# First chunk of six column groups ahead of the rest, a shorter look-ahead, and a row moved out of a load buffer

## The chip, the cores and the metric

The kernel runs on one core of one Trainium2 chip. The metric is the device time of one execution in microseconds (us). A core has five engines with instruction streams of their own that work in program order and wait for each other by semaphores: TensorE (PE in the profile, PEld its weight loads), VectorE (DVE), ScalarE (ACT), GpSimd (POOL) and SyncE (SP), which here issues all transfers.

## The reference, cut to what matters

One decoder layer in float32: a sequence of 256 rows, width 2048. The change lies in the first lines of it: the conditioning vector `c` gives a shift and a scale, the normalised input times the scale plus the shift is `h`, and `h` is multiplied with a wide matrix of which the kernel takes fourteen groups of 512 columns first.

```python
def hybrid_layer(x, c, w_ada, b_ada, norm_pre_w, w_in, ...):
    shift, scale, gate = jnp.split(jax.nn.silu(c) @ w_ada + b_ada, 3, axis=-1)
    h = rms_norm(x, norm_pre_w) * (1.0 + scale[:, None]) + shift[:, None]
    proj = h @ w_in
    (gdn_qkv, gdn_a, gdn_b, gdn_z, ml_qk, ml_v, ml_i, ml_f, ml_o, ml_z, gate_a, gate_b) = jnp.split(
        proj, np.cumsum(IN_SPLITS)[:-1].tolist(), axis=-1)
    ...
    merged = jax.nn.sigmoid(gate_a) * y_a + jax.nn.sigmoid(gate_b) * y_b
    out = merged @ w_out
    return x + gate[:, None] * rms_norm(out, norm_post_w)
```

## The kernel before

**Three products for one.** Each float32 operand is split into a rounded part and a rest (`split`, L167: ACT casts the rounded part, `whi`, L168; DVE or POOL subtracts it from the original to give the rest, `wlo`, L169). `mm3` (L215) then issues three matmuls of 512 columns: `h_hi` with `whi`, `h_hi` with `wlo`, `h_lo` with `whi`. `split_w` (L173) gives four of five subtractions of the start to POOL, the fifth to DVE.

**The stream.** `Stream` (L62) holds units in the order in which they were added. A unit is a load (one or two transfers into one of three buffers `raw` of 128 x 2048 numbers), its pieces of up to 1024 columns to be prepared (`prep_w`, L183), and their use on PE. `run` prepares pieces as long as no more than `ahead` (3) of them are prepared and not yet used, then issues the use of the oldest. As every engine works in program order, this also fixes what stands behind what on ACT, DVE and POOL. A load is issued as soon as the buffer three units before it is done with.

**The start.** The width 2048 is 16 chunks of 128 (index `k`). The row of `c` is loaded into one partition of a buffer of the ring `ar` (`crow`, L263), goes through Silu on ACT, and four PE matmuls spread it over all partitions (`csil`, L272). The input `x` lies in `xs`; its two halves of 128 rows are squared, summed and scaled by the root (`x_scale`, L289, ACT), and each pair of chunks is turned by four PE transposes and copied back by ACT (`x_turn`, L293, tile `xps`). For each chunk two rows blocks of `w_ada` (for the shift and the scale; 32 units of 1 MB, three buffers `ar`) are multiplied with `csil` and summed by DVE (L344). With both sums `h_chunk(k)` (L319) makes `sh`, `s1`, `hf` and `h_hi` on ACT and `h_lo` on POOL.

**The fourteen groups.** Their products with all 16 chunks are made in five blocks of chunks, `BLOCKS = ((0, 2), (2, 2), (4, 4), (8, 4), (12, 4))`, as first chunk and count. Within a block each group in turn gets its matmuls into two of four PSUM banks (`jtile`, L209, tiles `pn`), one for each half of 128 rows. After the first block ACT copies the two banks to `part[g]` (L403), after a later one DVE adds them to it (L405). In a block of two chunks one unit of 1 MB holds two groups. `PACE` says how many `w_ada` units are added before a block's first and last unit. In the stream the first ten chunks of `x` are turned ahead of the first group (`x_chunks(0, 6)` and `x_chunks(6, 10)`), the other six between later units. What comes after the fourteen groups is not touched by the change.

Of the kernel before, what the change touches and what calls it, by code (L numbers as in the profile page):

```python
# [7 lines left out]
F32 = mybir.dt.float32  # L8
F32R = mybir.dt.float32r
AF = mybir.ActivationFunctionType  # L10
ALU = mybir.AluOpType
# [105 lines left out]
def hybrid_layer_kernel(  # L117
# [91 lines left out]
    def jtile(nm):  # L209
        return pj.tile([P, 512], F32, name=nm, tag="pj")  # L210
# [49 lines left out]

    pcs = ExitStack()
    csil = pcs.enter_context(tc.tile_pool(name="pcs", bufs=1, space=PSUM)).tile([P, D], F32, name="csil")
    crow = sp.tile([P, D], F32, name="crow", tag="ar", bufs=ADA_BUFS)[0:1]  # L263
    SP.dma_start(crow, c_row)
    for b in range(2):
        SP.dma_start(xs[:, b], x[b * P:(b + 1) * P])
    SP.dma_start(ident, consts[:, 0:128])
    bat = const("bat", b_ada_t, [P, 32])
    npre = const("npre", npre_t, [P, KC])
    A.activation(crow, crow, AF.Silu)  # L270
    for q in range(4):
        T.matmul(csil[:, q * 512:(q + 1) * 512], one_row, crow[:, q * 512:(q + 1) * 512], start=True, stop=True)  # L272
    late_c = {}

    def late_consts():
# [25 lines left out]
    def x_chunks(k0, k1):  # L301

        x_scale(k0)
        for k in range(k0, k1, 2):
            if k + 2 < k1:
                x_scale(k + 2)
            x_turn(k)
    x_chunks(0, 6)


    bnp = sp.tile([P, KC], F32, name="bnp")
# [7 lines left out]
    def h_chunk(k):  # L319

        A.activation(sh[:, k:k + 1], ad[:, k:k + 1], AF.Identity, bias=bat[:, k:k + 1])
        A.activation(s1[:, k:k + 1], ad[:, KC + k:KC + k + 1], AF.Identity, bias=bnp[:, k:k + 1],
                     scale=npre[:, k:k + 1])
        hf = sp.tile([P, S], F32, name="hf", tag="hf", bufs=2)
        A.activation(hf.rearrange("p (b t) -> p b t", b=2), xs[:, :, k * P:(k + 1) * P], AF.Identity, bias=sh[:, k:k + 1], scale=s1[:, k:k + 1])
        split(hf, h_hi[:, k], h_lo[:, k], G)

    stream = Stream(load_w, side)
    BLOCKS = ((0, 2), (2, 2), (4, 4), (8, 4), (12, 4))
    PACE = (4, 9.5, 16.5, 26, 32, 32)  # L330
    due = []

    def h_chunks(k):

        while due and due[0] <= k:
            h_chunk(due.pop(0))

    def ada_units():

        adders = []  # L340
        for k in range(KC):
            for pt in range(2):
                def prep(h, raw, k=k, pt=pt):
                    V.scalar_tensor_tensor(raw, raw, 1.0, csil, op0=ALU.mult, op1=ALU.mult,  # L344
                                           accum_out=ad[:, pt * KC + k:pt * KC + k + 1])
                    if 4 <= 2 * k + pt < 8:
                        j = 2 * (2 * k + pt)
                        if j > 8:
                            x_turn(j)
                        if j < 14:  # L350
                            x_scale(j + 2)
                    h_chunks(k - 1)
                    if pt == 1:
                        due.append(k)
# [24 lines left out]
        G.memset(y0, 0.0)  # L379

    def add_start_groups(bi):
        k0, nk = BLOCKS[bi]
        lastb = bi == len(BLOCKS) - 1
        adders, parts_ = [], []
        for g in range(len(START)):
            st_ = {}

            def use(h, hi, lo, g=g, st_=st_):
                if h == 0:
                    st_["ps"] = [jtile(f"pn{i}") for i in range(2)]  # L390
                for kc in range(min(2, nk - 2 * h)):
                    kr = h * 2 + kc
                    k = k0 + kr
                    h_chunks(k)
                    o = kc * 512
                    for b in range(2):
                        mm3(st_["ps"][b], h_hi[:, k, b * P:(b + 1) * P], h_lo[:, k, b * P:(b + 1) * P],
                            hi[:, o:o + 512], lo[:, o:o + 512], kr == 0, kr == nk - 1)

            def after(g=g, st_=st_):  # L400
                for b in range(2):
                    if bi == 0:
                        A.copy(part[g][:, b], st_["ps"][b])  # L403
                    else:
                        V.tensor_tensor(part[g][:, b], st_["ps"][b], part[g][:, b], op=ALU.add)  # L405
                if bi == len(BLOCKS) - 2 and g == 3:
                    late_consts()
                if lastb:
                    pt = part[g].rearrange("p b c -> p (b c)")
                    A.activation(pt, pt, AF.Silu if g in (9, 11, 13) else AF.Sigmoid)  # L410
                    if g < 8:
                        SP.dma_start(gate_dr[g], part[g])
                    elif g % 2:
                        V.tensor_tensor(part[g], part[g], part[g - 1], op=ALU.mult)
                        SP.dma_start(gate_dr[8 + (g - 8) // 2], part[g])
                    if g == NG - 1:
                        branches_open()
            parts_.append((w_in[START[g]][:, k0 * 512:(k0 + nk) * 512], use, after))
        if nk == 2:
            for g in range(0, NG, 2):  # L420
                def use2(h, hi, lo, g=g):
                    parts_[g + h][1](0, hi, lo)
                    parts_[g + h][2]()
                adders.append(lambda g=g, use2=use2:
                              stream.add((parts_[g][0], parts_[g + 1][0]), prep_w, use2))
        else:
            for src, use, after in parts_:
                adders.append(lambda src=src, use=use, after=after:
                              stream.add(src, lambda h, raw: prep_w(h, raw, nk * 512), use, (nk + 1) // 2, after))
        return adders  # L430


# [72 lines left out]
        stream.add(w_ab, prep_w, use, after=lambda: side.add(gates(st_["ps"])))  # L505

    ada = ada_units()
    NG = len(START)
    ia = 0
    for bi, (k0, nk) in enumerate(BLOCKS):  # L510
        if bi == len(BLOCKS) - 1:
            add_ab()
        fs = add_start_groups(bi)
        for j, f in enumerate(fs):
            ahead = PACE[bi] + (PACE[bi + 1] - PACE[bi]) * j / len(fs)
            while ia < len(ada) and ia < ahead:
                ada[ia]()
                ia += 1
            f()
# [795 lines left out]
```

## Time and profile before

| what | value |
|---|---|
| time, median of 3 runs | 1634.56 us (1633.07 to 1636.01) |
| the profiled execution, its own time | 1634.3 us |
| its span, first to last instruction | 1632.5 us |
| PE busy | 1595.8 us, 98% of the span |
| ACT, DVE, POOL busy | 57%, 70%, 15% of the span |
| granted TensorE clock, mean | 0.997 |

The span is 1.8 us shorter than the time of the same execution; the rest lies outside the instructions. A busy share is that of an engine over the whole span; idle time of an engine matters only where the chain that ends last runs through it. In the rows further down, a row of the timeline has the start and the duration of an instruction in us, and in brackets how long the engine sat idle before it and who ended that. Matmuls are pipelined: the duration of one is longer than the distance to the next, and it is the distance that counts.

### The profile page before, as it was taken

The page shows a single profiled execution, that of the slowest core. Times are in us where ns is not written, and L with a number is a line of the kernel's source. Part 1 is how long each engine was busy: PE and PEld are TensorE (multiplying, and loading weights), DVE is VectorE, ACT ScalarE, POOL GpSimd, SP SyncE. Part 2 cuts the span into 40 slices and gives each one's busy share as a digit, 9 for nine tenths or more (in the row PEclk, how much of TensorE's full clock was granted, in tenths as well). Part 3 has the DMA queues.
Part 4 walks back from the last instruction along what each step waited for, and adds up shares of the span by engine and source line. Part 5 has one row for each costly group of instructions (what it writes and reads, how often), then busy time and mean ns, then how long its engine had stood idle before and what let it go on. Part 6 is the DMA issues. An engine that isn't in the chain of part 4 may idle for free.

```text
span 1632.5 us, 25436 instructions
## 1 busy us (share of the span) xinstructions
PE 1595.8 (98%) x9844; PEld 1398.7 (86%) x9844; DVE 1137.3 (70%) x1793; ACT 937.5 (57%) x1496; POOL 241.7 (15%) x191
## 2 busy tenths in 40 slices
PE   6999999999999999999999999999999999999997
PEld 4888887799998999999898989889988788888886
DVE  5585556665678787969686969685878556756654
ACT  7744446665655575666666666665565544444443
POOL 3877760000000010000000000000100000100101
PEclk9999999999999999999999999999999999999999
DMA  9998775765454555454546464646888668766572
GB/s 370 387 364 321 280 272 180 259 245 187 166 197 165 183 175 185 165 184 160 185 161 197 162 198 152 193 167 247 299 301 310 236 235 301 275 233 252 194 278 103
DMA packets 96259, 372.37 MB, mean 228 GB/s; under 512 B 26261, under 2 KB 46213, under 8 KB 58249
## 3 DMA queue, kind: packets, MB, share of 16 engines
q1 hardware_dynamic: 96138, 370.75, 63.9%
q8 instruction: 77, 1.26, 0.3%
q14 instruction: 44, 0.36, 0.1%
HBM read 354.40 MB, written 16.31 MB: 227 GB/s over the span
## 4 chain that ended last, share of the span: by engine, by line
PE 78%; issue 13%; DVE 3%; ACT 2%; DMA 2%; POOL 1%; SPq 0%; DVEq 0%; POOLq 0%; ACTq 0%
PE pn L217 34%; PE pt L217 27%; PE py L217 8%; DVE wlo L169 1%; ACT whi L168 1%; POOL mg L1123 1%; PE psa L217 1%; DMA raw<-in_dram 1%; PE mq L766 1%; PE mz L774 1%; PE mp L741 1%; PE pt L848 0%; DMA ar<-in_dram 0%; PE po L811 0%; PE pc L801 0%
## 5 line engine op out<-in xcount | busy, mean ns | idle before, releaser
L169 DVE TENSOR_TENSOR wlo<-raw,whi 128x1024 fp32r<-128x1024 f32 x450 | 552.7, 1237 | 273.3 <-ACT whi L168 272.4
L168 ACT CAST whi<-raw 128x1024 fp32r<-128x1024 f32 x514 | 532.0, 1051 | 313.2 <-PE pn L217 145.7
L217 PE MATMUL pt<-h_hi,whi 128*128 128x256 f32 x1280 | 368.1, 288 | 0.0
L217 PE MATMUL pt<-h_hi,wlo 128*128 128x256 f32 x1280 | 362.6, 283 | 1.9 <-DVE wlo L169 1.9
L217 PE MATMUL pt<-h_lo,whi 128*128 128x256 f32 x1280 | 362.0, 283 | 0.0
L217 PE MATMUL pn<-whi,h_hi 128*128 128x512 f32 x896 | 354.3, 395 | 3.5 <-ACT whi L168 3.4
L217 PE MATMUL pn<-wlo,h_hi 128*128 128x512 f32 x896 | 350.5, 391 | 3.0 <-DVE wlo L169 3.0
L217 PE MATMUL pn<-whi,h_lo 128*128 128x512 f32 x896 | 350.4, 391 | 0.0
L217 PEld LDWEIGHTS pt<-h_hi,wlo 128*128 128x128 f32 x1280 | 245.1, 191 | 2.8 <-DVE wlo L169 2.7
L217 PEld LDWEIGHTS pt<-h_hi,whi 128*128 128x128 f32 x1280 | 245.2, 192 | 1.3
L217 PEld LDWEIGHTS pt<-h_lo,whi 128*128 128x128 f32 x1280 | 245.3, 192 | 0.2
L217 PEld LDWEIGHTS pn<-whi,h_hi 128*128 128x128 f32 x896 | 169.1, 189 | 40.1 <-ACT whi L168 3.8
L217 PEld LDWEIGHTS pn<-wlo,h_hi 128*128 128x128 f32 x896 | 169.2, 189 | 38.4 <-DVE wlo L169 4.3
L217 PEld LDWEIGHTS pn<-whi,h_lo 128*128 128x128 f32 x896 | 169.0, 189 | 35.8 <-POOL h_lo L169 0.3
L169 POOL TENSOR_TENSOR wlo<-raw,whi 128x1024 fp32r<-128x1024 f32 x64 | 153.6, 2408 | 44.2 <-ACT whi L168 44.2
L217 PE MATMUL py<-whi,yhi 128*128 128x512 f32 x384 | 150.6, 392 | 0.3 <-ACT vt L953 0.3
L217 PE MATMUL py<-whi,ylo 128*128 128x512 f32 x384 | 149.5, 389 | 0.0
L217 PE MATMUL py<-wlo,yhi 128*128 128x512 f32 x384 | 149.4, 389 | 0.0
L405 DVE TENSOR_TENSOR part<-pn,part 128x512 f32<-128x512 f32 x112 | 74.0, 687 | 48.0 <-PE pn L217 48.0
L168 ACT CAST yhi<-ya 128x512 fp32r<-128x512 f32 x48 | 29.9, 622 | 124.7 <-PE py L217 122.9
L169 DVE TENSOR_TENSOR ylo<-ya,yhi 128x512 fp32r<-128x512 f32 x48 | 33.2, 692 | 90.4 <-ACT yhi L168 88.4
L567 DVE SCALAR_TENSOR_TENSOR qs<-pt,gcv,qs 128x255 f32<-128x255 f32 (+2 forms) x192 | 92.2, 480 | 4.6
(243 smaller groups left out, 1800.5 us busy)
## 6 DMA issues: line engine op xcount, KB each, us to landing
raw<-in_dram SPq DMA_DIRECT2D x259, 1024.0 KB
ar<-in_dram SPq DMA_DIRECT2D x32, 1024.0 KB
raw<-in_dram SPq DMA_DIRECT2D x28, 512.0 KB
ya<-o_dr SPq DMA_DIRECT2D x32, 256.0 KB
gate_dr<-part SPq DMA_DIRECT2D x11, 512.0 KB
gb<-rows SPq DMA_DIRECT2D x20, 256.0 KB
ug<-ud SPq DMA_DIRECT2D x32, 128.0 KB
o_dr<-oT SPq DMA_DIRECT2D x16, 256.0 KB
```

Source lines behind the costliest of these rows:

```text
L168: A.copy(hi, src)
L169: (eng or V).tensor_tensor(lo, src, hi.bitcast(F32), op=ALU.subtract)
L217: T.matmul(ps, l, r, start=start and i == 0, stop=stop and i == 2, skip_group_check=True)
L405: V.tensor_tensor(part[g][:, b], st_["ps"][b], part[g][:, b], op=ALU.add)
L567: V.scalar_tensor_tensor(dst[:, n, sh:], src[:, 0:S - sh], taps(n, 3 - sh), dst[:, n, sh:], op0=ALU.mult, op1=ALU.add)
L741: T.matmul(pss[t][o:o + 32, m * 32:(m + 1) * 32], um(m)[r:r + 32, o:o + 32], yc[r:r + 32, m], start=True, stop=True)
L766: T.matmul(psp[64:128, m * 64:(m + 1) * 64], um(m)[0:64, 64:128], y0[:, m], start=True, stop=True)
L774: T.matmul(psz[0:64, m * 64:(m + 1) * 64], p2[64:128, m], x0[64:128, m, 64:128], start=True, stop=True)
L1123: G.tensor_tensor(mcols(b, hf, cg), mcols(b, hf, cg), s_, op=ALU.add)
```

## The change

The fourteen groups are cut into six (`EARLY`) and eight (`REST`), and the first two blocks are replaced by four: the six with chunk 0 alone, the eight with chunks 0 and 1, the six with chunks 1 to 3, the eight with chunks 2 and 3. The later three blocks stay. Units with one or two chunks hold two groups (0.5 or 1 MB), the six with three chunks one group (0.75 MB). The last two numbers of a block stand in the place of `PACE`. `Stream` starts with `ahead` 1 and goes to 3 with the first use in the second block. The row of `c` goes to two partial-sum tiles instead of an `ar` buffer, as two transfers and two Silus. Four chunks of `x` are turned ahead of the first group instead of ten, the other twelve between later units. The rest `h_lo` of chunk 0 is made on DVE. In the first use of a group, one of the two PSUM copies goes to DVE for all but the first two groups.

```diff
-    crow = sp.tile([P, D], F32, name="crow", tag="ar", bufs=ADA_BUFS)[0:1]
-    SP.dma_start(crow, c_row)
+    crow = [part[4 + i].rearrange("p b c -> p (b c)")[0:1] for i in range(2)]
+    for i in range(2):
+        SP.dma_start(crow[i], c_row[:, i * 1024:(i + 1) * 1024])
...
-    A.activation(crow, crow, AF.Silu)
+    for i in range(2):
+        A.activation(crow[i], crow[i], AF.Silu)
...
-    x_chunks(0, 6)
+    x_chunks(0, 4)
...
-        split(hf, h_hi[:, k], h_lo[:, k], G)
-
-    stream = Stream(load_w, side)
-    BLOCKS = ((0, 2), (2, 2), (4, 4), (8, 4), (12, 4))
-    PACE = (4, 9.5, 16.5, 26, 32, 32)
+        split(hf, h_hi[:, k], h_lo[:, k], V if k == 0 else G)
+
+    stream = Stream(load_w, side, 1)
+    NG, NE = len(START), 6
+    EARLY, REST, ALL = range(NE), range(NE, NG), range(NG)
+
+    BLOCKS = ((EARLY, 0, 1, 1.1, 3.5), (REST, 0, 2, 4, 8), (EARLY, 1, 3, 8, 12), (REST, 2, 2, 12, 16.5),
+              (ALL, 4, 4, 16.5, 26), (ALL, 8, 4, 26, 32), (ALL, 12, 4, 32, 32))
...
-                    if 4 <= 2 * k + pt < 8:
-                        j = 2 * (2 * k + pt)
-                        if j > 8:
+                    j = 2 * (2 * k + pt) - 4
+                    if 2 <= j < 16:
+                        if j > 2:
                             x_turn(j)
...
                         if k == 0:
                             h_chunks(0)
-                            x_chunks(6, 10)
...
+        def after(g, ps):
+            for b in range(2):
+                if k0:
+                    V.tensor_tensor(part[g][:, b], ps[b], part[g][:, b], op=ALU.add)
+                elif g < 2 or b == 0:
+                    A.copy(part[g][:, b], ps[b])
+                else:
+                    V.tensor_copy(part[g][:, b], ps[b])
...
+        per = 1 if nk > 2 else 2
+        for g in groups[::per]:
...
+            def use_piece(h, hi, lo, g=g, st_=st_):
+                for i in range(min(2, per * nk - 2 * h)):
+                    gg, c = g + (2 * h + i) // nk, (2 * h + i) % nk
+                    if c == 0:
+                        st_["ps"] = [jtile(f"pn{i}") for i in range(2)]
+                    use(gg, st_["ps"], c, hi, lo, i * 512)
+                    if c == nk - 1:
+                        after(gg, st_["ps"])
+                if bi == 1:
+                    stream.ahead = 3
```

How the instructions move is shown at three places. On SP, the first loads before, from the first `ar` on (`ar` is a unit of `w_ada`, `raw` one of the groups' columns):

```order
L316 DMA ar<-in_dram 128x2048
L316 DMA ar<-in_dram 128x2048 [waits DMAHW0_49]
L316 DMA ar<-in_dram 128x2048 [waits DMAHW1_49,PE_49,Activation_49]
L316 DMA ar<-in_dram 128x2048 [waits DMAHW2_49,DVE_49]
L163 DMA raw<-in_dram 128x1024 [waits DMAHW3_49]
L163 DMA raw<-in_dram 128x1024 [waits DMAHW4_49]
```

And the same place now:

```order
L319 DMA ar<-in_dram 128x2048 [waits DMAHW0_49]
L319 DMA ar<-in_dram 128x2048 [waits DMAHW1_49]
L163 DMA raw<-in_dram 128x512 [waits DMAHW2_49]
L163 DMA raw<-in_dram 128x512 [waits DMAHW3_49]
L163 DMA raw<-in_dram 128x512 [waits DMAHW4_49]
L163 DMA raw<-in_dram 128x512 [waits DMAHW5_49]
L319 DMA ar<-in_dram 128x2048 [waits DMAHW6_49]
```

The first columns stand behind two units of `w_ada` instead of four, and the third unit waits no longer for PE. On ACT, before, from the cast of the first columns to the copies of the first group (`pn_253` and `pn_254` are its two banks; between the casts stand the parts of the second chunk of `h`):

```order
L168 CAST whi<-raw 128x1024 [waits DMAHW3_49]
L168 CAST whi<-raw 128x1024 [waits DMAHW4_49]
L291 ACTIVATE xs<-xs,rsx 128x256 x2
L321 ACTIVATE sh<-ad,bat 128x1 [waits DVE_49]
L322 ACTIVATE s_102<-ad,bnp,npre 128x1 [waits DVE_49]
L325 ACTIVATE hf<-xs,sh,s_102 128x256 [waits Activation_49]
L168 CAST h_hi<-hf 128x256 [waits Activation_49]
L168 CAST whi<-raw 128x1024 [waits DMAHW6_49]
L168 CAST whi<-raw 128x1024 [waits DMAHW7_49]
L403 COPY part_104<-pn_253 128x512 [waits PE_49]
L403 COPY part_104<-pn_254 128x512 [waits PE_49]
```

And now, from the third cast of columns on:

```order
L404 COPY part_105<-pn_216 128x512 [waits PE_49]
L168 CAST whi<-raw 128x1024 [waits DMAHW7_49,DMAHW0_49]
L404 COPY part_106<-pn_235 128x512 [waits PE_49]
L404 COPY part_107<-pn_245 128x512 [waits PE_49]
L294 ACTIVATE xs<-xs,rsx 128x256 x2
L168 CAST whi<-raw 128x1024 [waits DMAHW2_49]
L404 COPY part_108<-pn_264 128x512 [waits PE_49]
L404 COPY part_109<-pn_274 128x512 [waits PE_49]
L168 CAST whi<-raw 128x1024 [waits DMAHW3_49,DVE_49]
L324 ACTIVATE sh<-ad,bat 128x1 [waits DVE_49]
L325 ACTIVATE s_102<-ad,bnp,npre 128x1 [waits DVE_49]
```

Four casts stood ahead of the first copy; now two do, and from the third on each cast stands behind copies of matmuls that PE has to finish first. On PE, now, where chunk 1 of `h` is first used (group 7, banks `pn_291` and `pn_292`) and the turns of `x` follow:

```order
L217 MATMUL pn_291<-whi,h_hi 128x512 [waits Activation_49]
L217 MATMUL pn_291<-wlo,h_hi 128x512
L217 MATMUL pn_291<-whi,h_lo 128x512 [waits Pool_49]
L217 MATMUL pn_292<-whi,h_hi 128x512
L217 MATMUL pn_292<-wlo,h_hi 128x512
L217 MATMUL pn_292<-whi,h_lo 128x512
L300 MATMUL xps<-con,xs 128x128 [waits DVE_49]
L300 MATMUL xps<-con,xs 128x128 x3
L300 MATMUL xps<-con,xs 128x128 [waits DVE_49,Activation_49]
```

Before, that place had one turn behind the first group and no second one:

```order
L217 MATMUL pn_254<-whi,h_lo 128x512
L297 MATMUL xps<-con,xs 128x128 [waits PE_49]
L297 MATMUL xps<-con,xs 128x128 x3
L217 MATMUL pn_282<-whi,h_hi 128x512 [waits PE_49]
```

The second turn follows the first at once and waits for an ACT instruction that stands behind the first one's copy.

## Rows read from the trace of the kernel before

**Rows 1.** The page: span, and the busy time of PE.

```profile
span 1632.5 us, 25436 instructions
PE 1595.8 (98%) x9844; PEld 1398.7 (86%) x9844; DVE 1137.3 (70%) x1793; ACT 937.5 (57%) x1496; POOL 241.7 (15%) x191
```

**Rows 2.** The chain of work that ended last, from 0 to 120 us: start, us, what.

```profile
22.14 11.00 DMA raw<-in_dram
...
43.39 76.68 PE pn L217 x337
```

**Rows 3.** Busy time in stretches of 5 us: length, then PE, PEld, DVE, ACT, POOL busy (and instructions), granted clock, DMA share, GB/s.

```profile
20.00:25.00 5.00, 1.64 (x6) 0.73 (x4) 4.77 (x5) 2.86 (x5) 0.00 (x0) 1.00 1.01 422
25.00:30.00 5.00, 4.54 (x12) 3.11 (x12) 2.77 (x3) 4.39 (x9) 3.78 (x3) 1.00 1.02 424
30.00:35.00 5.00, 5.00 (x26) 4.15 (x25) 2.30 (x2) 4.52 (x9) 4.73 (x3) 1.00 1.02 424
```

**Rows 4.** What PE waited for from 20 to 290 us: us in total, times, longest.

```profile
PE pn L217 <- ACT whi L168: 3.4, 1, 3.4
PE pn L217 <- DVE wlo L169: 2.1, 2, 1.7
...
PE pn L217 <- ACT part L403: 0.2, 1, 0.2
```

**Rows 5.** Timeline, the first transfers on SP.

```profile
1.19 0.33 SPq L264 DMA_DIRECT2D crow<-in_dram  x1
1.56 0.82 SPq L266 DMA_DIRECT2D xs<-in_dram  x2
4.08 10.90 SPq L316 DMA_DIRECT2D ar<-in_dram  x4
```

**Rows 6.** Timeline of the engines up to the first matmuls of the groups.

```profile
12.32 2.29 DVE L344 SCALAR_TENSOR_TENSOR ar<-ar,csil 128x2048 f32<-128x2048 f32 x1 [1.46 <-DMA ar<-in_dram]
...
17.02 0.39 ACT L322 ACTIVATE s<-ad,bnp,npre 128x1 f32<-128x1 f32 x1 [0.63 <-DVE ar L344]
...
18.08 0.40 ACT L168 CAST h_hi<-hf 128x256 fp32r<-128x256 f32 x1
18.39 1.70 ACT L291 ACTIVATE xs<-xs,rsx 128x256 f32<-128x256 f32 x4
...
23.18 1.04 ACT L168 CAST whi<-raw 128x1024 fp32r<-128x1024 f32 x1 [1.59 <-DMA raw<-in_dram]
...
24.27 0.80 PE L217 MATMUL pn<-whi,h_hi 128*128 128x512 f32 x1 [3.36 <-ACT whi L168]
...
25.53 0.80 PE L217 MATMUL pn<-wlo,h_hi 128*128 128x512 f32 x1 [0.46 <-DVE wlo L169]
...
28.90 0.63 PE L217 MATMUL pn<-whi,h_lo 128*128 128x512 f32 x1
...
29.33 0.47 PE L217 MATMUL pn<-whi,h_hi 128*128 128x512 f32 x1
```

**Rows 7.** Timeline of PE around one turn of `x`, in the dense part.

```profile
35.78 0.39 PE L217 MATMUL pn<-whi,h_lo 128*128 128x512 f32 x1
...
36.02 0.60 PE L297 MATMUL xps<-con,xs 128*128 128x128 f32 x4
...
36.37 0.48 PE L217 MATMUL pn<-whi,h_hi 128*128 128x512 f32 x1
...
36.68 0.40 PE L217 MATMUL pn<-wlo,h_hi 128*128 128x512 f32 x1
```

**Rows 8.** Timeline of ACT in the dense part: a cast of 1024 columns, two PSUM copies, the copy of a turn, the next scaling.

```profile
35.13 1.06 ACT L168 CAST whi<-raw 128x1024 fp32r<-128x1024 f32 x1
36.08 1.08 ACT L403 COPY part<-pn 128x512 f32<-128x512 f32 x2
37.03 0.62 ACT L299 COPY xs<-xps 128x512 f32<-128x512 f32 x1
37.51 0.94 ACT L291 ACTIVATE xs<-xs,rsx 128x256 f32<-128x256 f32 x2
```

**Rows 9.** Groups of POOL instructions, 25 to 110 us: count, busy us, mean ns, idle before.

```profile
L169 POOL TENSOR_TENSOR wlo<-raw,whi 128x1024 fp32r<-128x1024 f32 x26 | 62.3, 2413 | 18.4 <-ACT whi L168 18.3
L169 POOL TENSOR_TENSOR h_lo<-hf,h_hi 128x256 fp32r<-128x256 f32 x7 | 5.3, 752 | 7.0 <-ACT h_hi L168 7.0
```

**Rows 10.** Timeline of DVE in the second block: four adds, then a unit of `w_ada`.

```profile
79.62 2.48 DVE L405 TENSOR_TENSOR part<-pn,part 128x512 f32<-128x512 f32 x4
82.02 2.28 DVE L344 SCALAR_TENSOR_TENSOR ar<-ar,csil 128x2048 f32<-128x2048 f32 x1
```

**Rows 11.** Timeline of PE around its two longest waits of the start.

```profile
285.61 0.50 PE L217 MATMUL pn<-wlo,h_hi 128*128 128x512 f32 x1 [1.68 <-DVE wlo L169]
...
286.18 0.40 PE L217 MATMUL pn<-whi,h_hi 128*128 128x512 f32 x1
286.41 0.39 PE L217 MATMUL pn<-wlo,h_hi 128*128 128x512 f32 x1
...
294.72 0.30 PE L488 MATMUL tp<-con,work 128*128 128x128 f32 x1 [3.60 <-DVE part L405]
...
296.42 0.63 PE L217 MATMUL pn<-wlo,h_hi 128*128 128x512 f32 x1
296.84 0.63 PE L217 MATMUL pn<-whi,h_lo 128*128 128x512 f32 x1
```

More of the change, by code (lines that the diff above doesn't have):

```diff
@@ L269, in hybrid_layer_kernel @@
     npre = const("npre", npre_t, [P, KC])
-    A.activation(crow, crow, AF.Silu)
+    for i in range(2):
+        A.activation(crow[i], crow[i], AF.Silu)
     for q in range(4):
-        T.matmul(csil[:, q * 512:(q + 1) * 512], one_row, crow[:, q * 512:(q + 1) * 512], start=True, stop=True)
+        T.matmul(csil[:, q * 512:(q + 1) * 512], one_row, crow[q // 2][:, (q % 2) * 512:(q % 2 + 1) * 512],
+                 start=True, stop=True)
     late_c = {}
@@ L381, in add_start_groups @@
     def add_start_groups(bi):
-        k0, nk = BLOCKS[bi]
+        groups, k0, nk = BLOCKS[bi][:3]
         lastb = bi == len(BLOCKS) - 1
-        adders, parts_ = [], []
-        for g in range(len(START)):
-            st_ = {}
[L388 to L429, printed above, removed]
+        def use(g, ps, c, hi, lo, o):
+            k = k0 + c
+            h_chunks(k)
+            for b in range(2):
+                mm3(ps[b], h_hi[:, k, b * P:(b + 1) * P], h_lo[:, k, b * P:(b + 1) * P],
+                    hi[:, o:o + 512], lo[:, o:o + 512], c == 0, c == nk - 1)
@@ new lines, in after @@
+        def after(g, ps):
+            for b in range(2):
+                if k0:
[4 more added lines that the diff above has]
+                    V.tensor_copy(part[g][:, b], ps[b])
+            if bi == len(BLOCKS) - 2 and g == 3:
+                late_consts()
+            if lastb:
+                pt = part[g].rearrange("p b c -> p (b c)")
+                A.activation(pt, pt, AF.Silu if g in (9, 11, 13) else AF.Sigmoid)
+                if g < 8:
+                    SP.dma_start(gate_dr[g], part[g])
+                elif g % 2:
+                    V.tensor_tensor(part[g], part[g], part[g - 1], op=ALU.mult)
+                    SP.dma_start(gate_dr[8 + (g - 8) // 2], part[g])
+                if g == NG - 1:
+                    branches_open()
@@ new lines, in add_start_groups @@
+        adders = []
+        per = 1 if nk > 2 else 2
+        for g in groups[::per]:
+            st_ = {}
+            def use_piece(h, hi, lo, g=g, st_=st_):
[8 more added lines that the diff above has]
+                    stream.ahead = 3
+            src = tuple(w_in[START[g + i]][:, k0 * 512:(k0 + nk) * 512] for i in range(per))
+            adders.append(lambda src=src, use_piece=use_piece:
+                          stream.add(src, lambda h, raw: prep_w(h, raw, per * nk * 512), use_piece,
+                                     (per * nk + 1) // 2))
@@ L507, in hybrid_layer_kernel @@
     ada = ada_units()
-    NG = len(START)
     ia = 0
-    for bi, (k0, nk) in enumerate(BLOCKS):
+    for bi, (groups, k0, nk, first, last) in enumerate(BLOCKS):
         if bi == len(BLOCKS) - 1:
@@ L514, in hybrid_layer_kernel @@
         for j, f in enumerate(fs):
-            ahead = PACE[bi] + (PACE[bi + 1] - PACE[bi]) * j / len(fs)
+            ahead = first + (last - first) * j / len(fs)
             while ia < len(ada) and ia < ahead:
```

## Prediction

> **What bounds the kernel now.** I read the page first: PE is busy for 1595.8 of 1632.5 us [rows 1], so only PE's idle time, some 37 us, and its slow matmuls can be won back. Then the chain of waits: from 43.39 us on it is PE itself, 337 matmuls in 76.68 us or 0.2275 us each; before that it runs through a load of columns from 22.14 us on [rows 2]. The stretches show where the idle time lies: PE is busy for 1.64 of 5 us from 20 to 25 us, for 4.54 in the next, and full from 30 us [rows 3]. The waits say that this is nearly all of the start: after the one wait of 3.4 us for the first cast, PE loses 0.2 us to a copy and 2.1 us to `wlo` up to 290 us [rows 4]. So the change can gain only ahead of some 30 us, and whatever it delays behind that point is lost in full, as PE has no slack there.
>
> One thing more about that place. The first matmul of a group starts at 24.27 us, the second at 25.53 us, and up to 29.33 us they follow each other at 0.43 us (28.90 to 29.33) instead of 0.2275 [rows 6]. That is 512 columns at the lower of TensorE's two levels (1.2 GHz), although the granted clock of the stretch reads 1.00 [rows 3]; PE had been mostly idle before.
>
> **The change part by part.**
>
> *The lead.* What ends last ahead of the first group is now the sum of the second `w_ada` unit, not the load of columns. Before, that sum let `s1` start at 17.02 us [rows 6]. The second transfer for the row of `c` costs SP one more issue, 1.56 - 1.19 = 0.37 us [rows 5], and all that follows, `x` and the two units, comes as much later: `s1` at 17.39. From `s1` to the end of `h_hi` it is 18.48 - 17.02 = 1.46 us, and the next ACT instruction starts 18.39 - 17.02 = 1.37 us after `s1` [rows 6]. That is now the cast of the first columns: 18.76 to 19.80 us. They are there in time: the first unit lands at 12.32, now 12.7; behind it the second (1.05 MB) and the columns (0.52 MB) take 3.8 us at some 410 GB/s, the rate at which the queue ran [rows 3], so they land at about 16.5. PE starts 1.09 us after a cast's start [rows 6], at **19.85**, a lead of 4.42 us on 24.27. The second matmul waits for DVE as before (1.26 us later): 21.11.
>
> *What is given back.* The first unit now holds 12 matmuls for one chunk of two groups, the next two units as many, then come units of 24. With `ahead` 1, only the first two pieces are cast before a copy; from the third on each cast stands behind copies on ACT that wait for PE, and its subtraction, nearly always POOL's (2.41 us [rows 9]), comes after that. I follow the order row by row. A cast moves ACT on by 0.95 us, a copy by 0.48, a turn's copy by 0.48, a scaling by 0.47 [rows 8]; a copy's result is there 0.55 after its start.
> - Batch 1: 11 more matmuls at 0.43 us from 21.11 end at 25.8. Its last copy ends at 26.6. The third cast runs to 27.65, POOL's subtraction from 27.7 to 30.1.
> - Batch 2, prepared long before, takes 12 x 0.2275 = 2.7 us: PE is through at 28.5, does one matmul of batch 3 and stands until 30.15: **1.4 us**. Batch 3 ends at 32.65.
> - Piece 4 is cast after two copies and two scalings, from 29.5, and subtracted from 30.6 to 33.0: **0.2 us**. Piece 5 is cast after two copies of batch 3 (32.7 to 33.7) and subtracted by POOL from 33.75 to 36.15.
> - Chunk 1 of `h` stands on ACT behind that cast: 0.2 us for `sh` and 1.46 for the rest give `h_hi` at 35.3. PE, with the six matmuls of chunk 0 done at 34.2, waits **1.1 us**. `h_lo` stands on POOL behind 36.15 and takes 0.75: 36.9; PE has done two more matmuls at 35.8 and waits **1.1 us** again. The piece ends at 37.85.
> - Two turns follow. The second needs a scaling that stands on ACT behind the copy of the first turn, itself behind a copy of the piece just ended: turn 38.3, copy 38.6 to 39.2, scaling from 39.1, second half of the wait at 39.65. PE stands **1.4 us**; the turns are through at 40.15 and PE starts its 49th matmul of the groups.
>
> From there each piece is cast two batches ahead and nothing waits. Before, 36 matmuls stood ahead of the turn at 36.02; the 37th started at 36.37, the 38th at 36.68 [rows 7], so the 49th at 36.68 + 11 x 0.2275 = 39.18. PE is 0.97 us late instead of 4.4 early.
>
> *The turns.* A turn costs dense PE (36.68 - 35.78) - 2 x 0.2275 = 0.45 us [rows 7]. Before, five lay in idle time and two more had passed at this point; now four have. Three more come later: **1.34 us**.
>
> *DVE in the second block of the eight.* A unit of 24 matmuls takes PE 5.46 us. DVE has four adds (2.40 us [rows 10]), 4.5 units of `w_ada` for four of columns (1.125 x 2.28 = 2.57) and about 0.45 of subtractions: 5.4 us, with no room; before it had one unit of `w_ada` for each. And at the seam two stand in a row ahead of a subtraction. Bounds: nothing, and the 1.68 us that PE once stood for such a subtraction at 285.61 [rows 11]. I take 0.5, nearer to nothing, since DVE enters this block with free time.
>
> *Costed at nothing.* The copies that go from ACT to DVE: DVE is busy for 2.3 of 5 us there [rows 3]; uncovered, 0.6 each. The third `w_ada` unit without its wait for PE: it is needed only for chunk 1, whose wait lies elsewhere. The two shorter Silus: `x` and its sums, not `csil`, end last. `h_lo` of chunk 0 on DVE: in the place of an idle 1.46 us [rows 6]; uncovered 0.4. The number of adds and copies stays.
>
> *Sum.* +0.97 + 1.34 + 0.5, less the 0.2 of [rows 4], is +2.6 us on the profiled execution's 1634.3: **1636.9 us**, against the median of 1634.56 +2.3, or 0.14%. A change under 0.2% (3.3 us) is about what cannot be told from none here.
>
> **The rivals.**
>
> *The clock falls again* (the one that ends slower). Between 28.5 and 40 us PE stands five times. If it went back to the lower level at the second stall, the rest of batch 3 would take 11 x 0.2 = 2.2 us more, which moves the copies, casts and subtractions behind it in full, and the six matmuls of the next piece about 1 us more, half hidden by the wait for chunk 1: +3.0, or **1639.9 us**. It decides with the first matmul after 30.15. For and against stand two waits: after 1.68 us of idle PE went on at 286.41 - 286.18 = 0.23 us a matmul, after 3.60 us it fell to 296.84 - 296.42 = 0.42 [rows 11]. The stalls are of at most 1.4 us, nearer to the first. [...]
>
> *The higher level comes early.* With all of batch 1 at 0.2275, it ends at 23.6, the third cast and all behind it move up by 2.2 us, and the time is **1634.7 us**. Against it: from rest PE took until 29.33 before.
>
> *The lead is kept.* If the stalls were covered, for example because a shorter way of the copies lets ACT cast ahead, what remains is 1634.3 - 4.42 + 1.34 - 0.2 = **1631.0 us**. Against it stands the order: the casts are behind the copies, whatever the durations.
>
> *DVE falls behind*: the upper bound of 1.7 instead of 0.5, **1638.1 us**. For it speaks the load of 5.4 in 5.46 us.
>
> **How the numbers follow.** Forecast 0.58 (alone 1635.0 to 1638.8: the steps of ACT and POOL are worth half a us each way, the point at which the clock rises about 1), the clock falls 0.15, early level 0.12, DVE 0.10, lead kept 0.05. The range leaves out the outer parts of the first and the last: 1632.8 to 1640.4. Slower by over 0.2%, above 1637.8: the clock case 0.14, DVE 0.07, a quarter of the forecast 0.15, together 0.36. Faster by over 0.2%, below 1631.3: 0.05. The same: 0.59.
>
> **What would show it.** The first matmul of a group near 19.9 us; a distance of 0.43 us until about 25 us; PE waiting for POOL's `wlo` near 30 us, for `h_hi` and `h_lo` near 35 and 37, for a scaling of `xs` near 39.5; the 49th matmul near 40; then no wait but one for DVE near 88. It is wrong if PE is dense from 28 us, if the distance goes back to 0.43 after 30 us, or if the load of columns ends the wait at 19.9 after all.

## The result and the profile after

| what | before | after |
|---|---|---|
| time, median of 22 runs each | 1635.71 us (1632.57 to 1642.82) | 1638.8 us (1636.38 to 1646.11) |
| ratio after to before | | 1.0019, 95% interval 1.0011 to 1.0028 |
| span of the profiled execution | 1632.5 us | 1637.1 us |

The changed kernel is 3.1 us slower by the medians, 0.19%. The interval, 0.11 to 0.28% or 1.8 to 4.6 us, leaves out zero: with 22 runs of each, a change under 0.2%, which the prediction took for one that cannot be told from none, can be told. The forecast was 1636.9 us, +2.6 on the profiled execution and +2.3 on the median known then, the range 1632.8 to 1640.4. The two executions that were profiled lie 4.6 us apart, more than the medians; where the other 1.7 us lie is told below.

The page of the changed kernel, span and PE, answers to [rows 1]:

```profile
span 1637.1 us, 25454 instructions
PE 1596.1 (97%) x9844; PEld 1398.8 (85%) x9844; DVE 1149.2 (70%) x1807; ACT 931.8 (57%) x1488; POOL 241.0 (15%) x192
```

PE does the same 9844 instructions in the same busy time (1596.1 against 1595.8 us). So what was lost is idle time of PE. What PE waited for from 20 to 290 us (us in total, times, longest) says where:

```profile
PE pn L217 <- ACT whi L168: 5.6, 1, 5.6
PE pn L217 <- DVE wlo L169: 2.1, 2, 1.7
PE pn L217 <- DVE part L402: 1.3, 1, 1.3
PE pn L217 <- POOL wlo L169: 1.1, 1, 1.1
PE xps L300 <- ACT xs L294: 1.1, 1, 1.1
PE pn L217 <- ACT h_hi L168: 1.0, 1, 1.0
PE pn L217 <- POOL h_lo L169: 0.9, 1, 0.9
```

Against [rows 4] five waits are new: for POOL's `wlo`, `h_hi`, `h_lo` and a scaling of `xs`, and one of 1.3 us for DVE's addition at L402 (L405 before). A last wait, of 0.4 us near 267 us, is left out here; every kernel of this document has it. The first row is the wait for the first cast; it ends 4.3 us earlier than before, which the length of the wait doesn't tell (it counts from the last turn, and fewer turns lie there now). The timeline shows when each ends (start, duration, idle time before and who ended it):

```profile
17.50 0.39 ACT L325 ACTIVATE s<-ad,bnp,npre 128x1 f32<-128x1 f32 x1 [2.14 <-DVE ar L350]
...
18.86 1.99 ACT L168 CAST whi<-raw 128x1024 fp32r<-128x1024 f32 x2
...
19.95 0.79 PE L217 MATMUL pn<-whi,h_hi 128*128 128x512 f32 x1 [5.64 <-ACT whi L168]
...
21.21 0.80 PE L217 MATMUL pn<-wlo,h_hi 128*128 128x512 f32 x1 [0.47 <-DVE wlo L169]
...
23.08 0.63 PE L217 MATMUL pn<-whi,h_lo 128*128 128x512 f32 x1
...
23.51 0.55 PE L217 MATMUL pn<-whi,h_hi 128*128 128x512 f32 x1
...
23.90 0.40 PE L217 MATMUL pn<-wlo,h_hi 128*128 128x512 f32 x1
24.13 0.39 PE L217 MATMUL pn<-whi,h_lo 128*128 128x512 f32 x1
...
25.05 0.40 PE L217 MATMUL pn<-whi,h_hi 128*128 128x512 f32 x1
...
25.73 1.05 ACT L168 CAST whi<-raw 128x1024 fp32r<-128x1024 f32 x1
...
26.86 2.39 POOL L169 TENSOR_TENSOR wlo<-raw,whi 128x1024 fp32r<-128x1024 f32 x1 [3.47 <-ACT whi L168]
...
29.30 0.50 PE L217 MATMUL pn<-wlo,h_hi 128*128 128x512 f32 x1 [1.13 <-POOL wlo L169]
...
34.58 0.50 PE L217 MATMUL pn<-whi,h_hi 128*128 128x512 f32 x1 [0.98 <-ACT h_hi L168]
...
36.17 0.49 PE L217 MATMUL pn<-whi,h_lo 128*128 128x512 f32 x1 [0.86 <-POOL h_lo L169]
...
38.88 0.83 PE L300 MATMUL xps<-con,xs 128*128 128x128 f32 x4 [1.08 <-ACT xs L294]
...
39.47 0.48 PE L217 MATMUL pn<-whi,h_hi 128*128 128x512 f32 x1
```

Four things are to be read here. `s1` at 17.50 and the first matmul at 19.95: the lead of 4.3 us is there, and the cast at 18.86 waits for nothing but `h_hi`, so the columns had landed. The distance from matmul to matmul is 0.43 us until 23.51 and 0.23 from 23.90 on: PE came to its higher level (2.4 GHz) some 4 us after the first matmul. Then four waits of 0.9 to 1.1 us, each ended by the engine that the prediction named. And behind each of them the matmuls go on at 0.23 us. The last row is the 49th matmul of the groups. Before, it was this one:

```profile
39.22 0.39 PE L217 MATMUL pn<-whi,h_hi 128*128 128x512 f32 x1
```

The prediction worked out 39.18 for it from [rows 7]. So 4.3 us of lead have become a delay of 0.25.

The fifth new wait, at the seam between two blocks:

```profile
82.34 2.29 DVE L350 SCALAR_TENSOR_TENSOR ar<-ar,csil 128x2048 f32<-128x2048 f32 x1 [0.50 <-DMA ar<-in_dram]
...
84.83 2.29 DVE L350 SCALAR_TENSOR_TENSOR ar<-ar,csil 128x2048 f32<-128x2048 f32 x1 [0.19 <-DMA ar<-in_dram]
...
86.12 1.05 ACT L168 CAST whi<-raw 128x1024 fp32r<-128x1024 f32 x1 [2.33 <-DMA raw<-in_dram]
...
87.20 1.22 DVE L169 TENSOR_TENSOR wlo<-raw,whi 128x1024 fp32r<-128x1024 f32 x1
...
87.52 0.39 PE L217 MATMUL pn<-whi,h_lo 128*128 128x512 f32 x1
88.34 2.48 DVE L402 TENSOR_TENSOR part<-pn,part 128x512 f32<-128x512 f32 x4
...
89.17 0.47 PE L217 MATMUL pn<-whi,h_hi 128*128 128x512 f32 x1 [1.26 <-DVE part L402]
```

PE loses 89.17 - 87.52 - 0.23 = 1.42 us. It waits for a bank, the bank for an addition that stands on DVE behind a subtraction, and that starts at 87.20: just as its cast ends, and just as DVE is through with two sums of `w_ada`. All three, the cast and both sums, had waited for a transfer.

In what follows two points serve as marks, since single runs scatter by several us: the 49th matmul of the groups, and the matmul behind the wait of 1.7 us for `wlo` that every kernel has near 285 us (285.61 in [rows 11], 288.55 now: +2.94). Behind that second mark 1.7 us of the 4.6 are still to come. Behind the 3.6 us of idle time of [rows 11] twelve matmuls run at the lower level in the changed kernel's profile (298.40 to 303.24, granted clock 0.50) and seven before (granted clock 0.50 as well), so that the sixteenth matmul behind it comes 4.18 us later than before, 304.40 for 300.22: 1.2 us more than at the mark. The last 0.4 lie far behind the change. As the medians lie 3.1 us apart, near the 2.94, I take this for scatter of the two executions.

### The profile page after: what moved, and what is told of

Same layout as the page of the kernel before. It is cut to its first block, busy times and chain, and to the rows that moved or that the text cites. A ratio compares the mean times of both kernels' runs of the same rounds, so it can differ in the third digit from the quotient of the medians.

```text
span 1637.1 us, 25454 instructions
## 1 busy us (share of the span) xinstructions
PE 1596.1 (97%) x9844; PEld 1398.8 (85%) x9844; DVE 1149.2 (70%) x1807; ACT 931.8 (57%) x1488; POOL 241.0 (15%) x192
## 3 DMA queue, kind: packets, MB, share of 16 engines
q8 instruction: 77, 1.26, 0.3%
## 4 chain that ended last, share of the span: by engine, by line
PE 76%; issue 13%; DVE 4%; DMA 3%; ACT 3%; POOL 2%; SPq 0%; DVEq 0%; ACTq 0%; POOLq 0%
PE pn L217 32%; PE pt L217 27%; PE py L217 8%; DVE wlo L169 1%; ACT whi L168 1%; DMA raw<-in_dram 1%; POOL mg L1131 1%; PE psa L217 1%; DMA ar<-in_dram 1%; DVE gacc L1030 1%; DMA ya<-o_dr 1%; PE mq L774 1%; PE mz L782 1%; PE mp L749 1%; PE pt L856 0%
## 5 line engine op out<-in xcount | busy, mean ns | idle before, releaser
L168 ACT CAST whi<-raw 128x1024 fp32r<-128x1024 f32 (+1 forms) x517 | 531.6, 1046 | 305.5 <-PE pn L217 134.0
L169 POOL TENSOR_TENSOR wlo<-raw,whi 128x1024 fp32r<-128x1024 f32 (+1 forms) x66 | 153.3, 2331 | 61.8 <-ACT whi L168 61.8
L402 DVE TENSOR_TENSOR part<-pn,part 128x512 f32<-128x512 f32 x112 | 73.7, 685 | 50.2 <-PE pn L217 50.1
```

Of the source, the lines that this page charges most:

```text
L402: V.tensor_tensor(part[g][:, b], ps[b], part[g][:, b], op=ALU.add)
```

## Experiments

All ratios are to the kernel before, run on the same chip in turn. The edits are against the changed kernel, but for e4.

| run | median, us | ratio (95%) | 49th matmul | wait near 88 us | second mark |
|---|---|---|---|---|---|
| before | 1635.4 to 1635.7 | 1 | 39.22 | none | 285.61 |
| after | 1638.8 | 1.0019 (1.0011 to 1.0028) | 39.47 | 1.26 | 288.55 |
| e1_ahead2 | 1637.06 | 1.0008 (0.9994 to 1.0022) | 38.16 | 0.82 | 287.12 |
| e2_pace | 1638.04 | 1.0020 (1.0011 to 1.0028) | 39.87 | none | 287.55 |
| e3_turn | 1639.73 | 1.0034 (1.0021 to 1.0047) | 38.77 | 0.32 | 289.48 |
| e4_row_only | 1636.2 | 1.0005 (0.9994 to 1.0015) | 39.30 | none | 285.83 |
| e5_two_on_dve | 1638.02, one run | | 39.25 | 0.69 | 288.95 |
| e6_ahead3 | 1637.0 | 1.0010 (0.9995 to 1.0025) | 38.28 | 0.33 | 286.43 |
| e7_chunk1 | 1634.27 | 0.9988 (0.9979 to 0.9997) | 35.54 | 1.65 | 284.98 |
| e8_chunk1_pace | 1632.95 | 0.9987 (0.9978 to 0.9997) | 35.62 | none | 283.16 |
| e9_chunk1_alone | 1643.61 | 1.0048 (1.0031 to 1.0064) | 43.45 | 0.4 | 291.67 |
| e10_all | 1633.34 | 0.9985 (0.9975 to 0.9996) | 35.44 | none | 282.90 |

**The look-ahead, e1 and e6.**

```diff
-    stream = Stream(load_w, side, 1)
+    stream = Stream(load_w, side, 2)      # e1; 3 in e6
```

> The changed kernel with a look-ahead of 2 instead of 1 up to the second block. Theory (the lead is given back because each cast stands behind copies that wait for PE): the waits for POOL's subtraction near 29 us and for the scaling of a turn near 38.9 us go, one wait for h_hi or h_lo of chunk 1 stays and is longer (about 2 us), the 49th matmul of the groups starts near 37.7 us instead of 39.47, and the time is 1.2 to 1.8 us below the changed kernel's, 1.3 to 1.9 above the kernel before. Rival (the pieces are late because their loads or POOL's rate hold them): 49th matmul at 39.2 or later, time as the changed kernel's.

The theory held in kind. In e1 the wait for POOL near 29 us is gone, and one wait takes the place of the other three:

```profile
34.76 0.50 PE L217 MATMUL pn<-whi,h_hi 128*128 128x512 f32 x1 [1.67 <-ACT h_hi L168]
35.10 0.39 PE L217 MATMUL pn<-wlo,h_hi 128*128 128x512 f32 x1
35.58 0.79 PE L217 MATMUL pn<-whi,h_lo 128*128 128x512 f32 x1
36.17 0.63 PE L217 MATMUL pn<-whi,h_hi 128*128 128x512 f32 x1
36.60 0.63 PE L217 MATMUL pn<-wlo,h_hi 128*128 128x512 f32 x1
```

Chunk 1 of `h` stands on ACT behind a turn's copy and two scalings (31.79 to 33.08 us). And behind this wait the distance goes back to 0.43 us (36.17 to 36.60), and the granted clock of the stretch (third number from the end) falls to 0.66:

```profile
35.00:40.00 5.00, 4.91 (x16) 3.68 (x16) 3.53 (x3) 3.64 (x7) 2.51 (x2) 0.66 1.02 415
```

The prediction's rival of the clock, which stayed out in the changed kernel, is there. The mark is 1.43 us ahead of the changed kernel's, the median 1.7 us below it.

> The changed kernel with a look-ahead of 3 pieces from the start instead of 1, as the kernel before had it. Theory: what eats the lead is the order on ACT, casts and the parts of chunk 1 of h against copies, and the long look-ahead is one more bad order of it: the four casts of the start stand ahead of the first copy, so that PE stands about 1.7 us for a bank, and chunk 1 comes later still, about 2.3 us of waiting near 37 us. The 49th matmul of the groups comes near 42.3 us instead of 39.47, the matmul behind the wait of 1.7 us near 288 comes at 291.3 instead of 288.55, and the time is 2.8 us longer than that of the changed kernel, about 1641. Rival, the short look-ahead itself costs the lead (each cast behind copies): with 3 the waits for POOL near 29 us and for the parts of chunk 1 go, the 49th matmul comes at or before 38 us, and the time is 1.5 us shorter or more.

Neither fits. The waits are where the theory put them, for banks that ACT empties late, but of 0.88 and 1.73 us, and the 49th matmul comes at 38.28, nearer to the rival. The parts of chunk 1 came earlier than I had them (`h_hi` at 33.18), so the longer look-ahead is not worse. With 3 the second mark is 288.55 - 286.43 = 2.1 us earlier, 1.2 of it ahead of the 49th matmul and 0.9 at the seam. So by the trace the short look-ahead, by itself, costs the changed kernel some 2 us. The medians of e1 and e6 are 1.7 and 1.8 us below the changed kernel's, but the intervals of their ratios overlap with its own, so the times alone don't settle it.

**The seam, e2.**

```diff
-(EARLY, 1, 3, 8, 12), (REST, 2, 2, 12, 16.5)
+(EARLY, 1, 3, 8, 13), (REST, 2, 2, 13, 16.5)
```

One more unit of `w_ada` goes ahead of the eight groups' second block, so one less lies between its columns. A unit is a transfer of 1 MB and DVE's sum of it; both move.

> The changed kernel with one more unit of w_ada spread over the six groups' second block (8 to 13) and one fewer in the eight groups' (13 to 16.5), so that no two units stand in a row at the seam. Theory (DVE's two sums in a row and full load hold the subtraction and the adds at the seam): the wait of 1.26 us for an add that ends at 89.17 us falls below 0.3, all else is the same, time 1.2 to 1.4 us below the changed kernel's. Rival (the load of columns that lands at 86.04 us ends that wait, because the transfers are behind): the cast at 86 us still waits for its load, a wait of PE of 0.8 us or more stays near 89 us, time within 0.6 of the changed kernel's.

From 60 to 283 us PE waits for nothing but the 0.4 us near 266 us that every kernel has. The same two engines at that place:

```profile
82.26 2.29 DVE L350 SCALAR_TENSOR_TENSOR ar<-ar,csil 128x2048 f32<-128x2048 f32 x1
...
84.37 1.05 ACT L168 CAST whi<-raw 128x1024 fp32r<-128x1024 f32 x1 [1.67 <-PE pn L217]
```

DVE's sum and the cast no longer wait for a transfer. The second mark is 1.00 us earlier though the 49th matmul was 0.40 later: 1.4 us, the whole wait. The time did not follow (ratio 1.0020 against 1.0019), so the times don't confirm the 1.4 us; the traces carry this point.

**The turns, e3 and e5.**

```diff
-    x_chunks(0, 4)
+    x_chunks(0, 6)
...
-                    if 2 <= j < 16:
-                        if j > 2:
+                    if 4 <= j < 16:
+                        if j > 4:
```

> The changed kernel with one more turn of x ahead of the first group (6 chunks instead of 4), where ACT and PE are idle, so that no turn follows another one in dense PE. Theory (each turn that leaves the idle stretch costs 0.45 us, and the second of a pair waits for ACT as well): the first matmul stays at 19.95 us, the wait of 1.08 us for the scaling near 38.9 shrinks to 0.7 or goes, the 49th matmul starts near 38.2 us, time 1.2 to 1.6 us below the changed kernel's. Rival (PE is through late by the waits for chunk 1 alone and the turns lie in their shadow): 49th matmul within 0.5 us of 39.47, time as the changed kernel's.

The theory fell. The pair of turns became one, as expected, and the 49th matmul came 0.7 us earlier. Then 2 us were lost where nothing had been before, and the median is 0.9 us above the changed kernel's instead of below it:

```profile
40.48 8.07 POOL L169 TENSOR_TENSOR wlo<-raw,whi 128x1024 fp32r<-128x1024 f32 x3 [3.94 <-ACT whi L168]
40.64 3.31 DVE L169 TENSOR_TENSOR wlo<-raw,whi 128x1024 fp32r<-128x1024 f32 x1
...
44.00 0.50 PE L217 MATMUL pn<-wlo,h_hi 128*128 128x512 f32 x1 [1.99 <-DVE wlo L169]
```

DVE's subtraction took 3.31 us instead of 1.22; in the changed kernel the same one had started at 40.21, ahead of POOL's at 41.19. For e5, e3 with one more piece on DVE:

```diff
-            split(src, hi, lo, G)
+            split(src, hi, lo, V if share[2] == 7 else G)     # share[2] counts the pieces
```

> e3_turn with one more piece: the seventh piece of columns is subtracted on DVE instead of POOL. In e3_turn DVE's subtraction of the sixth piece started at 40.64 us, 0.16 us behind a subtraction of POOL's that had started at 40.48, and took 3.31 us instead of 1.22; PE stood 1.99 us for it, until 44.00. Theory, one at a time: of two subtractions that both read SBUF, the one of DVE and the one of POOL, the later one stands until the earlier one is through (40.48 + 2.40 = 42.88, then 1.1 us). With no POOL subtraction at that point both DVE rows take 1.22 us and end at about 41.9 and 43.1, and the wait at 44.00 falls to at most 0.2 us. A turn close behind it may then wait in its place for a scaling, about 1 us. The Trainium skill, page SBUF - State Buffer, section SBUF: two separate sides, speaks for this theory: VectorE and GpSimd share a pair of ports that one holds for a whole instruction. Rival, something else at that place (transfers, a cast on ACT) makes the DVE row long: one of the two DVE rows still takes over 2 us and PE still waits for it, near 44 us, by over 1 us.

The theory held:

```profile
41.12 2.36 DVE L169 TENSOR_TENSOR wlo<-raw,whi 128x1024 fp32r<-128x1024 f32 x2
...
43.20 4.90 POOL L169 TENSOR_TENSOR wlo<-raw,whi 128x1024 fp32r<-128x1024 f32 x2 [6.17 <-ACT whi L168]
```

Two subtractions in 2.36 us, and the wait of 1.99 us is gone. What followed was a wait of 0.71 us for a copy on DVE at 46.34 instead of one for a scaling. It ran once, so its time decides nothing.

**The row alone, e4**: the kernel before with the part of the change that moves the row of `c`, nothing else.

> The kernel before with one part of the change alone: the row of c in two partial-sum tiles, as two transfers and two Silus. Theory (the third unit of w_ada waits no longer for PE's spread of c, so that it and the loads behind it land earlier, and nothing is given back): the first matmul of a group starts 0.7 to 2 us earlier than 24.27 us, PE is dense from there as before, time 0.7 to 2 us below the kernel before. Rival (the transfers are bound by their rate, the earlier issue only lengthens the queue): first matmul within 0.4 us of 24.27, no difference in time.

The third `w_ada` sum came 2.4 us earlier (17.07 for 19.45), the fourth 0.23 (21.75), the first matmul 0.24 (24.03): the transfers ran at 427 GB/s from 10 to 16 us and the columns come behind all four units. The rival was right; by itself this part shows no gain.

**Chunk 1, e7 and e9.**

```diff
-                        if k == 0:
-                            h_chunks(0)
+                        if k <= 1:
+                            h_chunks(k)
```

e9 is this edit alone, e7 has the look-ahead of 2 with it.

> The changed kernel with a look-ahead of 2 (as e1_ahead2) and with the parts of chunk 1 of h placed right behind the sum of the unit that completes it, instead of at the next unit. In e1_ahead2 PE stood 1.67 us for h_hi of chunk 1, until 34.76, and fell to the lower level behind it. Theory: chunk 1 stood late only because of its place on ACT, behind a turn's copy and two scalings; its sum was there before 27 us. Placed early, that wait goes, and with it the slow matmuls at 36 us: the 49th matmul comes near 35.3 us instead of 38.16 (39.18 in the kernel before), with short waits of 0.2 to 0.5 us near 29 to 33; the wait near 88 us for DVE's copy stays, 0.6 to 1.4 us; the matmul behind the 1.7 us wait comes near 284.6 (285.61 before), and the time is 1 us below the kernel before, ratio 0.9994. Rival, the 1.46 us of ACT only change places: the casts of the third to fifth piece come as much later, PE stands 1.5 us or more for POOL's wlo near 29 to 33 us, and the 49th matmul stays at 37 or later.

> The changed kernel with the parts of chunk 1 of h placed right behind the sum of the unit that completes it, and nothing else: the look-ahead stays at 1. Theory: the place of chunk 1 pays only with a look-ahead of 2. With 1, that sum stands on DVE behind copies that wait for PE, so sh would stand on ACT until some 31 us with the next casts behind it; the third to fifth pieces come later still, PE stands 1.5 to 2 us at two more places between 33 and 37 us and 1.4 us for a turn, the 49th matmul comes near 42.8 us (39.47 in the changed kernel, 35.54 with a look-ahead of 2), the matmul behind the 1.7 us wait near 291.9, and the time is some 3 us above the changed kernel. Rival: the place of chunk 1 is the whole cure and the look-ahead counts little: the waits near 35 and 37 us for h_hi and h_lo go, the 49th matmul comes at 37.5 or before.

Both theories held: 35.54 for an expected 35.3, and 43.45 for 42.8. With a look-ahead of 1 the same edit is a loss, because ACT then stands for a sum that is itself behind copies on DVE, and the casts behind ACT:

```profile
29.88 0.28 ACT L324 ACTIVATE sh<-ad,bat 128x1 f32<-128x1 f32 x1
32.21 0.39 ACT L325 ACTIVATE s<-ad,bnp,npre 128x1 f32<-128x1 f32 x1 [2.05 <-DVE ar L350]
...
37.09 0.79 PE L217 MATMUL pn<-wlo,h_hi 128*128 128x512 f32 x1 [1.93 <-POOL wlo L169]
```

Part of this execution's delay is the clock's: the first matmul at 0.23 us came 6.9 us after the first matmul of the groups (4.0 in the changed kernel), and six matmuls behind the last row ran at 0.43 us. The loss does not rest on that one execution: the medians lie 4.8 us apart, and the intervals of the two ratios do not meet.

In e7, e1's long wait and its slow matmuls are gone; short ones of 0.15 and 0.66 us are left. e7 is the first version faster than the kernel before.

**Together, e8 and e10**: e7 with the edit of e2, and that with the edit of e3.

> e7_chunk1 with the one unit of w_ada moved as in e2_pace (13 instead of 12 ahead of the eight groups' second block). Theory: the two cures add up, since they lie 50 us apart: the 49th matmul near 35.3 us, no wait of PE between 60 and 280 us, the matmul behind the 1.7 us wait near 283.6, which is 2 us ahead of the kernel before, ratio 0.9988. Rival: as PE is now 3 us earlier while the transfers come at the same rate, the columns are late instead and a wait for a load takes the place of the one that is cured, 1 us or more between 60 and 100 us; then 284.6 or later.

> e8_chunk1_pace with the first turns as in e3_turn: six chunks of x turned ahead of the first group, so one turn less in the dense part. Theory: it gains the 0.45 us of one turn (the two scalings and the turn lie in the idle time ahead of 19 us): the 49th matmul near 34.9 us (35.62 in e8), the matmul behind the 1.7 us wait near 282.7 (283.16 in e8), the time 0.5 us below e8, which the measurement cannot tell from none. Rival: as in e3_turn the scaling and copies that move on ACT bring a subtraction on DVE in behind one of POOL's that has just begun, and PE stands for it 1 to 2 us between 38 and 46 us: the matmul behind the 1.7 us wait at 284 or later.

What PE of e8 waits for from 12 to 330 us:

```profile
PE pn L217 <- ACT whi L168: 5.6, 1, 5.6
PE tp L497 <- DVE part L402: 3.6, 1, 3.6
PE pn L217 <- DVE wlo L169: 2.2, 2, 1.7
PE xps L300 <- ACT xs L294: 1.2, 1, 1.2
PE pab L217 <- POOL h_lo L169: 0.4, 1, 0.4
```

All five new waits of the changed kernel are gone (the 1.2 us for `xs` lie ahead of the first group). The second mark is 285.61 - 283.16 = 2.45 us ahead of the kernel before, the median 2.5 us below it, ratio 0.9987, or 0.03 to 0.22% faster. By the times e8 can't be told from e7 (0.9988); the 1.8 us between their marks rest on the traces. The theory held, and the wait for a load that the rival feared did not come. In e10 the mark is another 0.26 us earlier (282.90 for an expected 282.7) and DVE's subtraction was not caught (1.22 us); its time can't be told from e8's.

## Why the prediction was right, step by step

**The lead** held within 0.1 us: `s1` 17.50 (17.39 forecast), first matmul 19.95 (19.85), second 21.21 (21.11), and the cast stood behind `h_hi`, not behind the load.

**What is given back** held in kind: the engines and the order of all four waits are as forecast, and e7 shows that they are the cause, since without them the 49th matmul comes 3.9 us earlier. The term was mis-sized: +0.97 forecast, +0.25 measured. The failed step is the one that let all of batch 1 run at 0.43 us until 25.8. The higher level came near 23.7, so batch 2 began at 25.05, and the third cast started at 25.73 instead of 26.6. From the first matmul to the start of batch 2 it took 5.10 us for a forecast of 5.95; from there to the 49th matmul 14.42 for 14.35. So behind batch 1 the forecast chain held to 0.1 us in sum and only stands earlier. (The profile's idle times of 0.9 to 1.1 us look shorter than the forecast's, because they count from the end of a matmul's 0.39 us and the forecast from the next one's place, 0.23 us behind its start; counted the forecast's way they are 1.29, 1.15, 1.02 and 1.32 us.) That was the rival "the higher level comes early", in part: it was priced at 2.2 us for all of batch 1 and came for its last five matmuls. The other runs suggest the same: in e2, with the same order up to there, the level rose 1.3 us later, and the 49th matmul came 0.40 later although the first came 0.34 earlier.

**The turns** cost as forecast: behind the 49th matmul stand four (45.05, 51.00, 56.91 and 62.81 us) where one stood before (41.95), and each takes dense PE (45.72 - 44.82) - 2 x 0.2275 = 0.45. From the 49th matmul to the second mark the changed kernel takes 249.08 us, the one before 246.39. The difference of 2.69 is the turns' 1.34 and the 1.42 of the seam, less 0.07.

**The seam** was mis-sized and its mechanism was wrong in part. Forecast was 0.5 us, for DVE without room but with free time as it enters the block. DVE was indeed behind, but because its sums had waited for their transfers, and the cast beside it had waited 2.33 us for its own. The prediction had a load of DVE in this place and left out that of the queue. From 60 to 70 us the kernel before kept the transfers going, the changed one did not (its row is the second; the DMA share is the last number but one):

```profile
60.00:70.00 10.00, 10.00 (x45) 8.29 (x45) 4.31 (x4) 8.54 (x14) 7.01 (x4) 1.00 1.00 402
60.00:70.00 10.00, 10.00 (x48) 8.29 (x47) 8.66 (x10) 6.61 (x12) 8.06 (x5) 1.00 0.76 289
```

From 70 to 80 us it was 1.01 and 0.91, and from 80 to 90 us the share is 1.01 in the changed kernel: the loads bunch up at the seam behind a stretch in which the queue had room. e2 moves one unit forward, its share is 0.91 and 0.96 from 60 to 80 us, and all of the wait is gone. As DVE's sum moves with the transfer, e2 does not part the two; that the transfers were late is read from the waits above. Whether the sums or the cast alone would have held PE can't be told, as they ended within 0.1 us of each other, in e7 too.

**The clock** did not fall in the changed kernel, after waits of up to 1.13 us; so the rival had no part in the result. But it fell behind the 1.67 us of e1, and in e9, where PE did a single matmul between waits of 1.54 and 1.93 us (granted clock 0.68 from 35 to 40 us). The Trainium skill, page TensorE: Matmul & The Clock Gate, section HAM oscillation, tells of a loop that waits 3 to 5 us for a transfer between short runs of matmuls and begins each run at the lower level. All of these waits are shorter, so the section decides nothing about them; the 3.6 us of idle time behind the second mark are of its kind, and there the level fell in the kernel before and in the changed one but not in e2.

**The sum** was +0.25 + 1.34 + 1.42 - 0.07 = 2.94 at the second mark, against a forecast of +2.6: two errors of 0.7 and 0.9 us that nearly cancelled. That the time came out within 0.2% of the kernel before, the case that the prediction held for the likeliest, is owed to that in part, and it is a near thing, as the interval reaches to 0.28%.

**What the change costs in its parts**, by the second mark of one execution each: the look-ahead of 1 instead of 2 costs 1.4 us (e1), the late place of chunk 1 then 2.1 (e7), the place of one unit of `w_ada` then 1.8 (e8). In e1's execution the clock stood at its lower level for longer than in the other two, which makes the first step look smaller and the second larger. With these three put right the same start gains 2.5 us (e8), so the loss lies in them; the 1.34 us of the turns stay a cost of it. The times show the whole clear of noise (1.0019 against 0.9987, with intervals apart); from one step to the next the intervals overlap.

## What to carry to other kernels

A head start is worth only what the engines behind it can follow: before counting it, walk the order of each engine from the first result on, and look for preparations that stand behind the outputs of the work they prepare. Settings that decide this order act together (chunk 1 placed early cost 3.1 us at the second mark alone and gained 2.1 beside a longer look-ahead), so undo them in pairs. Where an engine looks overloaded, see first whether its own instructions wait for transfers.

## What the runs showed of the hardware

**DVE and POOL subtract one at a time.** A subtraction of 1024 columns that starts on DVE while POOL is in one takes up to 3.31 us instead of 1.22 (e3), and runs through once POOL has none (e5). The time it stands is inside the row's duration and counts as busy, not as a wait. The changed kernel has such rows too, 2.09 us at 51.09 behind one of POOL's from 49.71. The Trainium skill, page SBUF — State Buffer, section SBUF: two separate sides, says it: the two engines share a pair of ports that is held for a whole instruction, and the other one blocks. The rows agree: in e3 POOL's ends at about 40.48 + 2.40 = 42.88, and DVE needs 1.1 us more, until 43.95; in the changed kernel POOL's ends at 49.71 + 2.39 = 52.10, and DVE's at 53.18. DVE's sums of `w_ada`, which have their second operand `csil` in PSUM, are not stretched: 2.28 us at 41.34 in the changed kernel, while POOL subtracts from 41.19 on.

**The clock's level does not follow from the length of one wait.** Behind the 1.67 us of e1 it fell (granted clock 0.66 from 35 to 40 us), behind the 1.73 us of e6 and the 1.99 us of e3 it did not (1.00 from 35 to 40 and from 40 to 45 us). After the same 3.6 us of idle time seven matmuls were slow in the kernel before, twelve in the changed one and none in e2 (granted clock 1.00 from 295 to 300 us):

```profile
296.66 0.30 PE L497 MATMUL tp<-con,work 128*128 128x128 f32 x1 [3.58 <-DVE part L402]
...
297.36 0.39 PE L217 MATMUL pn<-wlo,h_hi 128*128 128x512 f32 x1
297.59 0.40 PE L217 MATMUL pn<-whi,h_lo 128*128 128x512 f32 x1
```

And from the first matmul of the groups to the first at 0.23 us it was 4.0 us in the changed kernel and 6.9 in e9, with the same start. The granted clock reads 1.00 from 20 to 25 us in both, so there only the distance shows the lower level. At 0.2 us a matmul this makes differences of 1 to 2.5 us between profiled executions. Each kernel has one profile, so whether two executions of one kernel differ as much, and what decides it, these runs don't show.
